# One transpose of x in place of two, with the row factors spread over the partitions

## The chip, the cores and the metric

The kernel runs on one core of a Trainium2 chip. The metric is device time in microseconds (us) of one execution; the time before is the median of 3 runs, 1371.86 us (1371.81 to 1372.82). In the profile PE is the matmul engine and PEld its weight loads, DVE, ACT and POOL are the vector, scalar and GpSimd engines, SP is the engine that issues the DMAs, and q behind an engine's name means its sequencer.

## The reference

One layer of a hybrid encoder: an adaLN-modulated RMSNorm, one wide input projection, sparse attention beside a Mamba-2 scan, a gated merge, and a SwiGLU feed-forward part. It is computed for 512 prompt rows and 64 sample rows of width 1024, 576 rows in all. What matters here is its very first step, and that x itself comes back at the first residual:

```python
mod = (jax.nn.silu(c) @ w_ada + b_ada)[:, None, :]
sh1, sc1, gt1, sh2, sc2, gt2 = jnp.split(mod, 6, axis=-1)
h = rms_normalize(x) * g_norm_mix * (1.0 + sc1) + sh1     # x * rsqrt(mean(x*x) + EPS) first
q, k, v, qi, ki, wi, z, xbc, dt, gate_logits = jnp.split(h @ w_in, offs, axis=-1)
...
x = x + gt1 * mixed
```

The shift and scale depend on the request group (prompt or sample) and on the channel; the factor 1/rms depends on the row.

## The kernel before

**How it is made.** The program is recorded, not issued at once: each call of `vec`, `act`, `pool`, `pe` or `sync` adds an operation to a plan (`Plan.add`, line 288), `Plan.order` (line 391) simulates all engines with a cost for each operation and takes, on each engine, the ready operation of the lowest priority number, and `Plan.emit` writes the operations out in that order. All instructions therefore carry the line of `emit`, 533; one goes by the names of the tiles. A block `with R.prio(n)` moves the priority of what is recorded in it. Each engine then works through its own list strictly in order, with semaphores between the lists.

**The layout.** The projection wants h with the channels on the partitions: `hTh` and `hTl`, 8 tiles of 128 channels x 576 rows each. They are the high and the low part of h, since every product is made of three fast fp32r matmuls (high x high, low x high, high x low). x comes in as five tiles `xt` with rows on the partitions, four of 128 rows and one of 64.

**The start, lines 802 to 893.** For each of the five tiles:

- ACT squares the tile into a scratch tile `xn` and sums the squares of each row into a column of `rs`. DVE multiplies by 1/1024 and adds EPS, POOL takes the power -1/2 (`rstd_of`). This gives the factor 1/rms of each row.
- DVE multiplies `xt` by the factor, into `xn` (two buffers).
- PE transposes the eight 128 x 128 blocks of `xn` into two PSUM tiles `px`, and ACT copies them to `xnT` (channels on partitions).
- Apart from that, PE transposes the eight blocks of the unscaled `xt` into a PSUM tile `mm` (two of them, two banks each), and DVE copies them to a tile `xs`. Six DMAs store these to `x_d` in DRAM, from where the first residual loads x much later. In the text this stands behind the making of h, with priority -1500.

So 40 blocks of `xn` and 40 blocks of `xt` are transposed.

**adaLN.** Four groups (`ada_pair`, j = 0 to 3) make shift and scale of 256 channels each. One needs four loads of 512 KB of `w_ada` (tiles `adr`, eight buffers, so that group j + 2 waits for the buffers of group j), 64 small matmuls into `py`, a copy `ra` on DVE, a transpose on PE, and the sums `modc` and `A` on DVE. `h_tile(kt)` then makes channel tile kt: `hu` = `xnT` * A + shift, on DVE for even kt and on ACT for odd kt, `hTh` is its rounded copy (ACT), `hTl` the rest (DVE, POOL for kt = 1 and 5):

```python
for j in range(4):
    ada_pair(j)
    fetch(0, EARLY[j])
    h_tile(2 * j)
    h_tile(2 * j + 1)
```

**Weights of the projection.** `fetch` loads slices of `w_in` into `raw` (two buffers); ACT makes the high part `wh`, DVE the low part `wl`, and a slice's buffer is loaded again when its `wl` is made. All these loads, those of `w_ada` and those of x stand in one list, SP's: the two small loads of c, the five of x, small rows, `w_ada` of group 0 (four), the first slice of `w_in` (the "misc" columns, in two pieces), `w_ada` of group 1, one slice, `w_ada` of group 2, two slices, `w_ada` of group 3, one slice. The first of the two slices between groups 2 and 3 goes into the buffer of the slice before group 2, so it waits for that one's `wl`.

**What PE does meanwhile.** As soon as channel tiles of h are there, PE begins the products of the first three slices (into `mm`, `px` and `py`), in pieces between the small matmuls of adaLN.

Of the kernel before, what the change touches and what calls it, by code (L numbers as in the profile page):

```python
# [5 lines left out]
F32 = mybir.dt.float32  # L6
F32R = mybir.dt.float32r
BF = mybir.dt.bfloat16
AF = mybir.ActivationFunctionType
OP = mybir.AluOpType  # L10
# [3 lines left out]
P = 128  # L14
D = 1024
NP_, NS = 512, 64
T = NP_ + NS
TH = T // 2
HP, HS = NP_ // 2, NS // 2
# [521 lines left out]
def build(tc, I, O):  # L541
    R = Plan(tc)
    vec, act, pool, pe, sync = R.vec, R.act, R.pool, R.pe, R.sync
# [5 lines left out]
    xsp = R.mkpool("xs", side="right")  # L549
    sp = R.mkpool("start")  # L550

    def pmm(name):
        return psum.tile([P, 2, 512], F32, name=name, tag="mm", bufs=2)

    def px(name, tag="px"):
        return psum.tile([P, 512], F32, name=name, tag=tag, bufs=2)
# [5 lines left out]
    ident = cp.tile([P, P], F32, name="ident")  # L562
# [129 lines left out]
    xt = []  # L692
    for tb in range(5):
        n = P if tb < 4 else NS
# [21 lines left out]
    sh1, sc1, gt1, sh2, sc2, gt2 = (modc[:, i] for i in range(6))  # L716
# [14 lines left out]
    def ada_pair(j):  # L731
# [15 lines left out]
        for w in range(2):  # L747
            vec.tensor_tensor(modc[:, w, 2 * j:2 * j + 2, :], p2[:, 64 * w:64 * w + 64].rearrange("p (g s) -> p g s", g=2)[:, :, 0:2],
                              badc[:, 8 * w + 2 * j:8 * w + 2 * j + 2, None].to_broadcast([P, 2, 2]), OP.add)
        vec.scalar_tensor_tensor(A1[:, 2 * j:2 * j + 2], sc1[:, 2 * j:2 * j + 2], 1.0, g_mix[:, 2 * j:2 * j + 2, None].to_broadcast([P, 2, 2]),  # L750
                                 op0=OP.add, op1=OP.mult)
# [39 lines left out]
    def rstd_of(ss, out, n, rows, denom):  # L791
        vec.tensor_scalar(out, ss, 1.0 / denom, EPS, op0=OP.mult, op1=OP.add)
        pow_mhalf(out, out, n)

    def bcast_rows(name, r5):

        pr = [px(name + "a"), px(name + "b", "py")]
        for tb in range(5):
            o = pr[0][:, tb * P:tb * P + P] if tb < 4 else pr[1][:, 0:P]
            pe.transpose(o, r5[:, tb:tb + 1].to_broadcast([P, P]), ident)  # L800
        return pr

    PARTS = ((0, 0, NP_), (1, NP_, NS))

    xnT = sp.tile([P, 8, T], F32, name="xnT")
    x_d = R.dram([P, 8, 2, TH], F32, name="x_d")
    rs = sp.tile([P, 5], F32, name="rs")
    pool.memset(rs, 1.0)
    for tb in range(5):
        n = P if tb < 4 else NS  # L810
        xn = sp.tile([P, D], F32, name=f"xn{tb}", tag="xn", bufs=2)
        act.activation(xn[:n], xt[tb][:n], AF.Square, accum_out=rs[:n, tb:tb + 1])
        rstd_of(rs[:n, tb:tb + 1], rs[:n, tb:tb + 1], 1, n, D)
        vec.tensor_scalar(xn[:n], xt[tb][:n], rs[:n, tb:tb + 1], None, op0=OP.mult)
        for k4 in range(2):
            p = px(f"pxn{tb}_{k4}")
            for j in range(4):
                kt = 4 * k4 + j
                pe.transpose(p[:, j * P:j * P + n], xn[:n, kt * P:(kt + 1) * P], ident[:n, :n])
            act.activation(xnT[:, 4 * k4:4 * k4 + 4, tb * P:tb * P + n], p.rearrange("p (k q) -> p k q", k=4)[:, :, :n], AF.Copy)  # L820
    rowsD = sp.tile([48, P], F32, name="rowsD")
    sync.dma_start(rowsD, I["b_ada"][0].rearrange("(a b) -> a b", b=P))
    badc = cp.tile([P, 48], F32, name="badc")
# [17 lines left out]
    stc = cp.tile([P, 3, 32], F32, name="stc")  # L841
    vec.tensor_scalar(bc_, vc[:, 32:64], 0.5, None, op0=OP.mult)

    A1 = cp.tile([P, 8, 2], F32, name="A1")
    hTh = hp.tile([P, 8, T], F32R, name="hTh")
    hTl = hp.tile([P, 8, T], F32R, name="hTl")
    hsS = hp.tile([P, 8, P], F32R, name="hsS")

    def h_tile(kt):
        u = sp.tile([P, T], F32, name=f"hu{kt}", tag="hu", bufs=3)  # L850
        for s, c0, n in PARTS:
            if kt % 2:
                act.activation(u[:, c0:c0 + n], xnT[:, kt, c0:c0 + n], AF.Identity, bias=sh1[:, kt, s:s + 1], scale=A1[:, kt, s:s + 1])
            else:
                vec.tensor_scalar(u[:, c0:c0 + n], xnT[:, kt, c0:c0 + n], A1[:, kt, s:s + 1], sh1[:, kt, s:s + 1], op0=OP.mult, op1=OP.add)
        act.activation(hTh[:, kt, :], u, AF.Copy)
        (pool if kt % 4 == 1 else vec).tensor_tensor(hTl[:, kt, :], u, hTh[:, kt, :].bitcast(F32), OP.subtract)

# [11 lines left out]
        act.activation(hsS[:, ks, 0:NS], hTh[:, ks, NP_:T].bitcast(F32), AF.Copy)  # L870
        act.activation(hsS[:, ks, NS:P], hTl[:, ks, NP_:T].bitcast(F32), AF.Copy)
    xst = []
    with R.prio(-1500):
        for tb in range(5):
            n = P if tb < 4 else NS
            p = pmm(f"pxt{tb}")
            for kt in range(8):
                pe.transpose(p[:, kt // 4, (kt % 4) * P:(kt % 4) * P + n], xt[tb][:n, kt * P:(kt + 1) * P], ident[:n, :n])
            st = xsp.tile([P, 8, P], F32, name=f"xs{tb}", tag="xs", bufs=5)
            for k4 in range(2):  # L880
                vec.tensor_copy(st[:, 4 * k4:4 * k4 + 4, :n], p[:, k4].rearrange("p (k q) -> p k q", k=4)[:, :, :n])
            if tb < 4:
                xst.append((x_d[:, :, tb // 2, tb % 2 * P:tb % 2 * P + P], st))
            else:
                for hf in range(2):
                    xst.append((x_d[:, :, hf, HP:TH], st[:, :, HS * hf:HS * hf + HS]))


    sync.dma_start(rowsB, I["w_conv"][0].rearrange("j (a b) -> (j a) b", b=P))
# [130 lines left out]
    p = px("pmiscT")  # L1020
# [3 lines left out]
    p = px("pmiscS")  # L1024
# [92 lines left out]
    p = px("pacs")  # L1117
# [11 lines left out]
    p = [px("pacsTa"), px("pacsTb", "py")]  # L1129
# [18 lines left out]
    for b in range(5):  # L1148
        n = P * (b + 1) if b < 4 else T
# [3 lines left out]
    for b in (4, 1, 2, 3):  # L1153
        smp = b == 4
        n = T if smp else P * (b + 1)
        rows = NS if smp else P
        k0 = NP_ if smp else 0
        s = ix.tile([P, n], F32, name=f"score{b}")
        for h in range(NIH // 2 if smp else NIH):
            q0 = 8 * NP_ + h * P if smp else h * NP_ + b * P  # L1160
            q = qis[:, q0:q0 + P]
# [101 lines left out]
    for kv in range(NKV):  # L1263
# [21 lines left out]
        for un in units + [None]:  # L1285
            nxt = None
            if un is not None:
                b, qs, k0, n, nk, v0, w = un
# [208 lines left out]
    for g in range(NG):  # L1497
# [4 lines left out]
        for i in range(4):  # L1502
# [9 lines left out]
            if 2 <= g < 6 and i > 1:  # L1512
                with R.prio(-600):
                    k = 2 * (g - 2) + i - 2
                    load_split(sd, o_d[:, k, :], oh[k], ol[k], 2)
    stage_c(NG - 1)
    for s, dst in ((0, O["conv_prompt"]), (1, O["conv_sample"])):
        p = px(f"pcvo{s}")
# [113 lines left out]
    for hf in range(2):  # L1632
# [4 lines left out]
        p = px(f"pss2{hf}")  # L1637
# [7 lines left out]
        pr = px(f"pr2{hf}", "py")  # L1645
# [175 lines left out]
    for i, (f, w, x, b, starts, *p) in enumerate(steps):  # L1821
# [198 lines left out]
    for o in order:  # L2020
        assert o in wd, o
        hi, lo = wd[o]
        if o[0] == "plain":
# [4 lines left out]
            for j in range(nk):  # L2028
                k = k0 + j
# [13 lines left out]
        else:  # L2043
            r, p = o[1:]
# [3 lines left out]
            bank_, q, starts = banks_d[r][b], DOWN[p][1], p in (1, 2, 7)  # L2048
# [49 lines left out]
```

## Time and profile before

| what | value |
|---|---|
| median of 3 runs | 1371.86 us |
| profiled execution: time, span | 1372.06 us, 1370.4 us |
| PE busy | 1351.5 us (99%) |
| PEld busy | 1312.5 us (96%) |
| DVE busy | 1112.8 us (81%) |
| ACT busy | 735.8 us (54%) |
| POOL busy | 250.8 us (18%) |
| moved by DMA | 200.70 MB, mean 146 GB/s |

The profiled execution is 0.2 us above the median of the runs, and 1.7 us of its time lie outside the span. A row of a timeline or chain gives the start and the duration in us, the engine, the operation with what it writes <- reads, and the number of instructions merged in the row; what stands in brackets is the idle time before it and what ended it. A row of windows gives, for a stretch of the span, its length, the busy time of each engine (with the number of instructions), the TensorE clock reported, the busy share of the DMA engines and the rate. A matmul's end is modelled, so the pace of PE is read from the distance of starts, not from the busy time.

### The profile page before, as it was taken

Reading aid. Unit: us, or ns where it says so; the run is one execution under the profiler, and the core shown is the slowest. Engines: PE = TensorE matmul, PEld = TensorE weight load, DVE = VectorE, ACT = ScalarE, POOL = GpSimd, SP = SyncE. Lnnn points to the kernel's source line nnn. Section 1 sums busy time; section 2 is a strip of 40 time slices with the busy share of each in tenths; the row PEclk is TensorE's granted clock in tenths of the full one; section 3 lists DMA queues with packets and bytes.
Section 4 is the critical chain, followed back from the end, with each engine's and each line's share of the span. In section 5 each row is a group of like instructions: output and inputs, shape, how many; then the busy total and the mean of one; then the engine's idle time right before and its main releaser. Section 6 shows DMA issues by size and latency. Waiting matters only on the chain.

```text
span 1370.4 us, 27779 instructions
## 1 busy us (share of the span) xinstructions
PE 1351.5 (99%) x10705; PEld 1312.5 (96%) x10705; DVE 1112.8 (81%) x2249; ACT 735.8 (54%) x1535; POOL 250.8 (18%) x376
## 2 busy tenths in 40 slices
PE   7999999999999999999999999999999999999998
PEld 5899999999999999999999999999999999999998
DVE  5688999787778698888897588868799998878564
ACT  5435343777876666666665342224576666664321
POOL 1312002230300245546453200001000000000000
PEclk9999999999999999999999999999999999999999
DMA  9762335574754644444445598757233343325431
GB/s 297 225 177 84 110 106 149 129 190 99 178 143 112 175 127 122 138 129 139 132 116 170 179 310 264 241 158 254 91 94 100 105 133 94 93 74 158 122 107 36
DMA packets 267764, 200.70 MB, mean 146 GB/s; under 512 B 25200, under 2 KB 239376, under 8 KB 267632
## 3 DMA queue, kind: packets, MB, share of 16 engines
q1 hardware_dynamic: 263680, 184.77, 46.0%
q0 software_dynamic: 3952, 14.16, 5.0%
q8 instruction: 84, 1.38, 0.4%
q14 instruction: 48, 0.39, 0.1%
HBM read 158.33 MB, written 29.55 MB: 137 GB/s over the span
## 4 chain that ended last, share of the span: by engine, by line
PE 86%; DVE 7%; DMA 4%; ACT 2%; issue 1%; SPq 1%; ACTq 0%; DVEq 0%
PE mm L533 61%; PE py L533 14%; PE px L533 11%; DMA stage<-y_d 2%; DVE score L533 1%; DMA raw<-in_w_in 1%; DVE m L533 1%; DVE wl L533 1%; SPq L533 1%; DMA xt<-in_x_sample 1%; DVE y L533 0%; ACT wh L533 0%; DVE xlS L533 0%; DMA rawu<-in_w_gate_up 0%; ACT wl L533 0%
## 5 line engine op out<-in xcount | busy, mean ns | idle before, releaser
L533 ACT ACTIVATE wh<-raw 128x1024 fp32r<-128x1024 f32 (+3 forms) x152 | 149.0, 983 | 181.4 <-PE mm L533 117.4
L533 PE MATMUL mm<-hTh,wh 128*128 128x288 f32 (+1 forms) x1024 | 235.5, 305 | 0.9 <-ACT hTh L533 0.9
L533 PE MATMUL mm<-hTh,wl 128*128 128x288 f32 (+1 forms) x1024 | 232.0, 301 | 0.0
L533 PE MATMUL mm<-hTl,wh 128*128 128x288 f32 (+1 forms) x1024 | 230.0, 301 | 0.4 <-DVE hTl L533 0.4
L533 PEld LDWEIGHTS mm<-hTh,wh 128*128 128x128 f32 (+1 forms) x1024 | 166.7, 188 | 3.9 <-ACT hTh L533 1.5
L533 PEld LDWEIGHTS mm<-hTh,wl 128*128 128x128 f32 (+1 forms) x1024 | 166.3, 188 | 2.7 <-issue 1.6
L533 PEld LDWEIGHTS mm<-hTl,wh 128*128 128x128 f32 (+1 forms) x1024 | 165.4, 188 | 3.3 <-issue 1.2
L533 DVE TENSOR_TENSOR wl<-raw,wh 128x1024 fp32r<-128x1024 f32 (+2 forms) x109 | 132.4, 1215 | 27.7 <-ACT wh L533 24.3
L533 DVE SCALAR_TENSOR_TENSOR cu<-xc,wc,cu 128x579 f32<-128x579 f32 x96 | 83.6, 870 | 2.1 <-ACT cu L533 1.6
L533 PE MATMUL mm<-wl,hTh 128*128 128x256 f32 x256 | 72.4, 284 | 0.0
L533 PE MATMUL mm<-wh,hTl 128*128 128x256 f32 x256 | 72.3, 284 | 0.0
L533 PE MATMUL mm<-wh,hTh 128*128 128x256 f32 x256 | 72.0, 284 | 0.0
L533 DVE SCALAR_TENSOR_TENSOR aacc<-adr,sil,aacc 128x512 f32<-128x512 f32 x84 | 59.8, 754 | 4.4 <-DMA adr<-in_w_ada 4.1
L533 PE MATMUL mm<-yh,wl 128*128 128x288 f32 x256 | 56.2, 298 | 0.0
L533 PE MATMUL mm<-yh,wh 128*128 128x288 f32 x256 | 55.2, 298 | 0.5 <-ACT yh L533 0.5
L533 PE MATMUL mm<-yl,wh 128*128 128x288 f32 x256 | 54.8, 296 | 0.6 <-DVE yl L533 0.6
L533 ACT ACTIVATE P<-lg,mn 128x128 f32<-128x128 f32 (+4 forms) x72 | 41.7, 581 | 25.2 <-DVE mn L533 24.0
L533 PE MATMUL mm<-xhS,wh 128*128 128x290 f32 (+1 forms) x248 | 55.2, 297 | 0.0
L533 PE MATMUL mm<-xhS,wl 128*128 128x290 f32 (+1 forms) x232 | 51.2, 296 | 0.0
L533 ACT ACTIVATE dec<-dec,nacs 128x128 f32<-128x128 f32 x128 | 42.5, 392 | 13.5 <-POOL dec L533 12.9
L533 PEld LDWEIGHTS mm<-wl,hTh 128*128 128x128 f32 x256 | 48.2, 189 | 0.4 <-issue 0.2
L533 PEld LDWEIGHTS mm<-wh,hTl 128*128 128x128 f32 x256 | 48.1, 188 | 0.3
(509 smaller groups left out, 3978.3 us busy)
## 6 DMA issues: line engine op xcount, KB each, us to landing
raw<-in_w_in SPq DMA_DIRECT2D x80, 512.0 KB, 4.0
adr<-in_w_ada SPq DMA_DIRECT2D x36, 512.0 KB, 5.2
raw<-in_w_gate_up SPq DMA_DIRECT2D x22, 512.0 KB, 3.8
wl<-raw POOLq DMA_DIRECT2D x21, 512.0 KB, 4.7
rawu<-in_w_gate_up SPq DMA_DIRECT2D x20, 512.0 KB, 3.9
bc<-acs_d SPq DMA_DIRECT2D x32, 256.0 KB, 3.6
raw<-in_w_branch_ssm SPq DMA_DIRECT2D x16, 512.0 KB, 4.5
raw<-in_w_down SPq DMA_DIRECT2D x16, 448.0 KB, 3.9
```

The costliest lines, as they stand in the source:

```text
L533: getattr(engines[x.eng], x.fn)(*[real(a) for a in x.args], **{k: real(v) for k, v in x.kw.items()})
```

## The change

x is transposed only once, unscaled, into `xT` (all 576 rows in one tile, in the pool that held `xs`). The squares go to a scratch tile `xsq` of one buffer. `bcast_rows` (line 795, which was there for another stage) transposes each column of `rs`, broadcast to 128 columns, on PE, so that every partition holds the 576 factors; ACT copies them from PSUM to `rB`. `h_tile` first multiplies the channel tile of `xT` by `rB`, on DVE, into `xr`. The six stores to `x_d` now read `xT`.

```diff
-    xnT = sp.tile([P, 8, T], F32, name="xnT")
+    xT = xsp.tile([P, 8, T], F32, name="xT")
+    xr = sp.tile([P, 8, T], F32, name="xr")
...
     for tb in range(5):
         n = P if tb < 4 else NS
-        xn = sp.tile([P, D], F32, name=f"xn{tb}", tag="xn", bufs=2)
-        act.activation(xn[:n], xt[tb][:n], AF.Square, accum_out=rs[:n, tb:tb + 1])
+        sq = sp.tile([P, D], F32, name=f"xsq{tb}", tag="xsq", bufs=1)
+        act.activation(sq[:n], xt[tb][:n], AF.Square, accum_out=rs[:n, tb:tb + 1])
         rstd_of(rs[:n, tb:tb + 1], rs[:n, tb:tb + 1], 1, n, D)
-        vec.tensor_scalar(xn[:n], xt[tb][:n], rs[:n, tb:tb + 1], None, op0=OP.mult)
+        p = pmm(f"pxt{tb}")
+        for kt in range(8):
+            pe.transpose(p[:, kt // 4, (kt % 4) * P:(kt % 4) * P + n], xt[tb][:n, kt * P:(kt + 1) * P], ident[:n, :n])
         for k4 in range(2):
-            p = px(f"pxn{tb}_{k4}")
-            for j in range(4):
-                kt = 4 * k4 + j
-                pe.transpose(p[:, j * P:j * P + n], xn[:n, kt * P:(kt + 1) * P], ident[:n, :n])
-            act.activation(xnT[:, 4 * k4:4 * k4 + 4, tb * P:tb * P + n], p.rearrange("p (k q) -> p k q", k=4)[:, :, :n], AF.Copy)
+            vec.tensor_copy(xT[:, 4 * k4:4 * k4 + 4, tb * P:tb * P + n], p[:, k4].rearrange("p (k q) -> p k q", k=4)[:, :, :n])
...
+    pr = bcast_rows("prx", rs)
+    rB = sp.tile([P, T], F32, name="rB")
+    act.activation(rB[:, 0:NP_], pr[0], AF.Copy)
+    act.activation(rB[:, NP_:T], pr[1][:, 0:NS], AF.Copy)
...
     def h_tile(kt):
+        vec.tensor_tensor(xr[:, kt], xT[:, kt], rB, OP.mult)
         u = sp.tile([P, T], F32, name=f"hu{kt}", tag="hu", bufs=3)
...
-                vec.tensor_scalar(u[:, c0:c0 + n], xnT[:, kt, c0:c0 + n], A1[:, kt, s:s + 1], sh1[:, kt, s:s + 1], op0=OP.mult, op1=OP.add)
+                vec.tensor_scalar(u[:, c0:c0 + n], xr[:, kt, c0:c0 + n], A1[:, kt, s:s + 1], sh1[:, kt, s:s + 1], op0=OP.mult, op1=OP.add)
...
-    with R.prio(-1500):
-        for tb in range(5):
-            n = P if tb < 4 else NS
-            p = pmm(f"pxt{tb}")
-            for kt in range(8):
-                pe.transpose(p[:, kt // 4, (kt % 4) * P:(kt % 4) * P + n], xt[tb][:n, kt * P:(kt + 1) * P], ident[:n, :n])
-            st = xsp.tile([P, 8, P], F32, name=f"xs{tb}", tag="xs", bufs=5)
-            for k4 in range(2):
-                vec.tensor_copy(st[:, 4 * k4:4 * k4 + 4, :n], p[:, k4].rearrange("p (k q) -> p k q", k=4)[:, :, :n])
-            if tb < 4:
-                xst.append((x_d[:, :, tb // 2, tb % 2 * P:tb % 2 * P + P], st))
-            else:
-                for hf in range(2):
-                    xst.append((x_d[:, :, hf, HP:TH], st[:, :, HS * hf:HS * hf + HS]))
+    for tb in range(4):
+        xst.append((x_d[:, :, tb // 2, tb % 2 * P:tb % 2 * P + P], xT[:, :, tb * P:tb * P + P]))
+    for hf in range(2):
+        xst.append((x_d[:, :, hf, HP:TH], xT[:, :, NP_ + HS * hf:NP_ + HS * hf + HS]))
```

More of the change, by code (lines that the diff above doesn't have):

```diff
@@ L852, in h_tile @@
             if kt % 2:
-                act.activation(u[:, c0:c0 + n], xnT[:, kt, c0:c0 + n], AF.Identity, bias=sh1[:, kt, s:s + 1], scale=A1[:, kt, s:s + 1])
+                act.activation(u[:, c0:c0 + n], xr[:, kt, c0:c0 + n], AF.Identity, bias=sh1[:, kt, s:s + 1], scale=A1[:, kt, s:s + 1])
             else:
-                vec.tensor_scalar(u[:, c0:c0 + n], xnT[:, kt, c0:c0 + n], A1[:, kt, s:s + 1], sh1[:, kt, s:s + 1], op0=OP.mult, op1=OP.add)
+                vec.tensor_scalar(u[:, c0:c0 + n], xr[:, kt, c0:c0 + n], A1[:, kt, s:s + 1], sh1[:, kt, s:s + 1], op0=OP.mult, op1=OP.add)
         act.activation(hTh[:, kt, :], u, AF.Copy)
```

## The prediction

> **What bounds the kernel now.** I read the page first, then the busy time in windows of 5 us, then the timeline, chain and waits of the first 50 us, the only place that the change touches.
>
> ```profile
> PE 1351.5 (99%) x10705; PEld 1312.5 (96%) x10705; DVE 1112.8 (81%) x2249; ACT 735.8 (54%) x1535; POOL 250.8 (18%) x376
> ```
>
> ```profile
> core 0: us, PE busy (x) PEld busy (x) DVE busy (x) ACT busy (x) POOL busy (x), PEclk, DMA share, GB/s
> 5.00:10.00 5.00, 3.83 (x17) 3.44 (x18) 2.17 (x5) 2.30 (x4) 0.64 (x2) 1.00 1.02 347
> 15.00:20.00 5.00, 3.77 (x53) 2.93 (x54) 3.18 (x8) 3.04 (x6) 1.10 (x2) 1.00 1.14 290
> 25.00:30.00 5.00, 3.68 (x46) 2.77 (x47) 1.63 (x5) 3.04 (x5) 1.41 (x1) 1.00 1.13 331
> 35.00:40.00 5.00, 4.46 (x53) 3.63 (x52) 2.30 (x7) 2.09 (x4) 0.00 (x0) 1.00 1.13 335
> 55.00:60.00 5.00, 5.00 (x44) 5.00 (x43) 4.29 (x11) 1.88 (x3) 1.53 (x2) 1.00 1.00 300
> ```
>
> PE is the bound: 19 us of the span are not PE's, and most of them lie in the first 45 us, where its windows hold 3.7 to 4.5 of 5 us. From 50 us on it is full, so what arrives there late or early by 1 us moves the end by 1 us. In the first 40 us it is the DMA engines that are full (share 1.02 to 1.14). Who waits for whom there:
>
> ```profile
> 5.38 1.54 PE L533 MATMUL mm<-ident,xt 128*128 128x128 f32 x6 [2.32 <-DMA xt<-in_x_prompt]
> 6.96 0.69 DVE L533 COPY xs<-mm 128x512 f32<-128x512 f32 x1 [3.14 <-PE mm L533]
> 7.71 3.04 PE L533 MATMUL mm<-ident,xt 128*128 128x128 f32 x13 [0.78 <-DVE rs L533]
> 13.71 1.04 PE L533 MATMUL px<-ident,xn 128*128 128x128 f32 x8
> 22.04 0.28 DVE L533 COPY ra<-py 128x128 f32<-128x128 f32 x1
> 22.34 1.02 DVE L533 TENSOR_TENSOR wl<-raw,wh 128x832 fp32r<-128x832 f32 x1
> 24.62 0.77 DVE L533 TENSOR_SCALAR hu<-xnT,A,modc 128x512 f32<-128x512 f32 x2
> 26.45 0.26 PEld L533 LDWEIGHTS mm<-hTh,wh 128*104 128x104 f32 x2 [0.81 <-ACT hTh L533]
> 27.82 1.07 PE L533 MATMUL py<-adr,sil 128*32 128x128 f32 x28
> 28.94 0.29 DVE L533 COPY ra<-py 128x128 f32<-128x128 f32 x1 [1.75 <-PE py L533]
> 29.81 1.23 DVE L533 TENSOR_TENSOR wl<-raw,wh 128x1024 fp32r<-128x1024 f32 x1 [0.58 <-ACT wh L533]
> 31.07 0.92 SPq L533 DMA_DIRECT2D raw<-in_w_in  x2
> 32.08 4.86 SPq L533 DMA_DIRECT2D adr<-in_w_ada  x4
> 37.41 0.43 PE L533 MATMUL mm<-hTh,wl 128*128 128x288 f32 x2
> 44.18 0.80 PEld L533 LDWEIGHTS py<-adr,sil 128*32 128x32 f32 x28 [0.18 <-DMA adr<-in_w_ada]
> 48.61 2.12 DVE L533 TENSOR_TENSOR hTl<-hu,hTh 128x576 fp32r<-128x576 f32 x2 [0.44 <-ACT hTh L533]
> 50.78 0.26 PEld L533 LDWEIGHTS mm<-hTl,wh 128*104 128x104 f32 x2 [0.42 <-DVE hTl L533]
> ```
>
> The stage ends when the last tiles of h are ready (48.61 to 50.73, PE waits for them at 50.78). They hang on the last load of the fourth w_ada group, which releases PE at 44.18. So what decides is when that load lands, not how soon x is transposed. Two rows of the chain and one of the page's list of issues tell how much air its queue has:
>
> ```profile
> 3.43 7.62 DMA xt<-in_x_sample
> 31.49 6.56 DMA raw<-in_w_in
> ...
> raw<-in_w_in SPq DMA_DIRECT2D x80, 512.0 KB, 4.0
> ```
>
> The slice issued at 31.49 lands at 38.05, 6.56 us later, against 4.0 us typical of such a load. It is the second of two issued together, and at some 340 GB/s (windows) the 512 KB ahead of it take 1.5 us. So 6.56 - 4.0 - 1.5 = 1.1 us of queue stand in front: the issue at 31.07 may come 1.1 us later before anything lands later; beyond that the delay reaches the four w_ada loads behind it, one for one.
>
> **The change, part by part.** As built, SP's list has the same loads in the same order. The lists of the other engines differ only up to the products and sums of w_ada's second group (about 30 us in the trace), apart from names. The six stores to x_d keep their place and their chunks of 512 and 128 bytes per row: 0.
>
> ```profile
> L533 PE MATMUL px<-ident,xn x40: 222/272/421, 10.5 to 22.7; 128*128 128x128 f32 x32, 64*128 64x64 f32 x8
> L533 ACT ACTIVATE xnT<-px x10: 378/594/598, 11.6 to 23.0; 128x512 f32<-128x512 f32 x8, 128x256 f32<-128x256 f32 x2
> L533 ACT ACTIVATE xn<-xt x5: 1047/1057/1057, 5.4 to 19.4; 128x1024 f32<-128x1024 f32 x4, 64x1024 f32<-64x1024 f32 x1
> L533 ACT ACTIVATION_READ_ACCUMULATOR xn<-xt x5: 187/190/202, 6.4 to 20.3; 128x1 f32 x4, 64x1 f32 x1
> L533 DVE TENSOR_SCALAR xn<-xt,rs x5: 743/745/754, 9.0 to 21.4; 128x1024 f32<-128x1024 f32 x4, 64x1024 f32<-64x1024 f32 x1
> L533 DVE COPY xs<-mm x10: 414/686/692, 7.0 to 17.6; 128x512 f32<-128x512 f32 x8, 128x256 f32<-128x256 f32 x2
> 33.23 1.43 DVE L533 TENSOR_TENSOR hTl<-hu,hTh 128x576 fp32r<-128x576 f32 x2 [1.04 <-ACT hTh L533]
> 7.80 0.57 POOL L533 TENSOR_TENSOR rs<-rs,mhalf 128x1 f32<-128x1 f32 x1 [5.55 <-DVE rs L533]
> ```
>
> Removed: 40 transposes on PE, 10 ACT copies (8 x 0.59 + 2 x 0.38 = 5.5 us) and 5 DVE products (5 x 0.75 = 3.7 us). Added: 5 transposes, two ACT copies (0.6 and some 0.25 us), 8 DVE products of 576 columns. The nearest row for these is hTl, also two SBUF operands of 576 columns: 1.43 us for two, so 5.7 us for eight. The ten DVE copies stay. DVE has 2 us more work and ACT about 4.7 us less, both far from full there. What counts is the chain, in which three things get later:
>
> 1. *The blocks of x.* A block of x used to be interleaved with transposes of xn. Now four of them follow each other, and in each the last two transposes wait until DVE has copied the first bank, as in the first block before: six from 5.38, copy 6.96 to 7.65, the rest from 7.71. PE's pace in these rows is (3.04 - 0.42) / 12 = 0.22 us a transpose at first and (1.04 - 0.27) / 7 = 0.11 from 13 us on, though the clock is given as 1.00 throughout (0.42 and 0.27 are the duration of one in each row). A block is 7.71 + 2 x 0.21 - 5.38 = 2.75 us at the slow pace, about 1.9 at the fast one. Four blocks from 5.38: 15.4 us if the pace doubles at 13.0 as before, 16.4 if it stays slow; the sample's half block and two small transposes: 16.0 or 17.5. x itself has long landed (11.05 by the chain), and the last of the five squares, 1.06 us and 0.19 for reading the sum, is done by 12.3.
>
> 2. *The factors.* All five must be there before any tile of h. The fifth stands on DVE behind the copies (16.0 or 17.2), POOL adds 0.57, then five transposes, an ACT copy of 0.6 and their handovers: 18.3 or 20.0. Then eight products, 5.7 us, which DVE does before `ra` of w_ada's first group: until 24.0 or 25.7. Before, `ra` was at 22.04. `ra`, the low part of the misc slice (1.0 us), `modc` and `A` follow: `hu` at 25.6 or 27.3, against 24.62.
>
> 3. *Who waits.* PE stands behind the transpose of `ra`, so the second group's matmuls queue there, though their data is in. `ra` of the second group comes at about 29.9 (before 28.94). If PE is still slow, then at about 32.8: `hu` at 27.3, 1.8 us to PE's first product (24.62 to 26.45), then 8 products and 32 small matmuls at twice their time. Products start 0.13 us apart (0.43 us for two of 0.30), the small ones 0.8 / 28 = 0.029 (1.07 us less the 0.27 of one), so 2.0 and 1.8 us. DVE makes the low part `wl` of the first full slice behind it, 1.23 us, and SP's issue of 31.07 waits for that: 31.4 or 34.3.
>
> The sum: 31.4 is 0.3 late, less than the 1.1 us of queue, so 0. 34.3 is 3.2 late, so 3.2 - 1.1 = 2.1 us reach the last w_ada load, the tiles of h and the end. If the pace doubles on the way, in the 20s, I get `ra` some 1.8 us late, with 0.7 us left over. Before shows both paces and one change between them, after some 5 us of nearly unbroken work; it does not show how PE behaves with a block's pauses of about 1 us. In the changed kernel an unbroken run comes only with the small matmuls of group 1 (64, about 20 to 23 us) or with the products from 27 on. I take +1.0 us, between these two. By the saved work nothing is gained: PE's 35 passes, ACT's copies and DVE's products all fall before 44 us, under the loads.
>
> [...]
>
> **The rivals.**
>
> *Faster: the transposes were on the path.* 35 passes fewer at 0.11 us are 3.8 us: 1371.86 - 3.8 = 1368.1 us. PE's fullness over the whole span speaks for it. Against it: PE waits for loads at 44.18, and the loads' order and bytes don't change. It would need DMA time to shrink.
>
> *Slower: the slow pace lasts into the full stage.* From 36 us on PE has hardly any idle time, and each us at half pace loses 0.5 us beside the 2.1. It decides, past 0.2%, if the pace doubles later than about 38 us; at 44 us it would be 2.1 + 0.5 x 8 = 6.1 us at most, less PE's idle time in the 35 to 40 window (0.5): about 5.5 us, 1377.4 us. For it: long pauses before 28 us. Against it: PE has unbroken work from 28 on, and before, 5 us of it were enough.
>
> *Nothing at all.* The pace doubles at 13 us as before, the queue's air takes up the 0.3 us: 1371.9 us.
>
> **How the numbers follow.** A measurement of this kernel can hardly tell less than 0.2% (2.7 us) from no change. Forecast, 0 to 2.1 us slower with the likeliest +1.0: 1372.9 us (its span by the profile 1371.4; the profiled execution took 1372.06, 0.2 above the median). Chance of the forecast with "nothing at all", which is its lower end: 0.84. Slower rival, of which I put the most just past 0.2%: 0.12. Faster rival: 0.04. The range: 1371.2 below (nothing at all, less what the runs scatter), 1374.9 above, 0.9 past the sum at slow pace, for the start of the slower rival. The same cases give faster 0.04, same 0.84, slower 0.12.
>
> **What would show it.** Right: PE's first transposes in blocks with pauses for DVE; eight `xr` products, one after the other, near 18 to 26 us; the first `hu` at 25 to 27.5; SP's pair of slices at 31.4 to 34.3; the release of PE by the last w_ada load at 44 to 46.3, and the wait for `hTl` at 50.8 to 52.9; the order and pace behind that as before. Wrong: if that load lands before 43.5 (a gain that I exclude); if `wl` of the first slice is past 35; if the stage after 53 us takes another time than before; or if transposes to strided rows of `xT` make DVE's copies longer than 0.69 us, at 0.1 us each 1 us more in step 2.

## The result, and the profile after

| | before | changed |
|---|---|---|
| median of the runs made together (8 each) | 1372.88 us (1371.81 to 1374.21) | 1377.32 us (1375.72 to 1378.77) |
| ratio, 95% interval | | 1.0032 (1.0021 to 1.0042) |
| profiled execution: time, span | 1372.06 us, 1370.4 us | 1377.31 us, 1375.5 us |

The change makes the kernel 4.4 us slower, and its time lies 2.4 us past the upper end of the range predicted (the kernel before, measured beside it, is 1.0 us above the median from which the forecast starts). The interval of the ratio lies clear of 1. PE's and DVE's busy times are within 1.3 us of what they were. From the page of the changed kernel, its first part:

```profile
PE 1352.2 (98%) x10670; PEld 1311.5 (95%) x10670; DVE 1114.1 (81%) x2252; ACT 732.5 (53%) x1527; POOL 250.8 (18%) x376
```

So the span has 4.4 us more in which PE isn't busy (23.3 us against 18.9). The windows of the changed kernel show where (length, busy time of PE, PEld, DVE, ACT and POOL, the granted clock, DMA share, GB/s):

```profile
20.00:25.00 5.00, 3.35 (x64) 2.70 (x56) 4.55 (x7) 1.20 (x2) 0.00 (x0) 1.00 1.10 344
25.00:30.00 5.00, 2.30 (x37) 1.47 (x39) 3.86 (x10) 2.60 (x5) 0.23 (x1) 0.73 1.12 332
30.00:35.00 5.00, 5.00 (x45) 3.81 (x46) 0.86 (x2) 0.63 (x1) 1.18 (x1) 0.59 0.50 160
35.00:40.00 5.00, 5.00 (x71) 3.73 (x73) 3.07 (x8) 3.13 (x6) 0.00 (x0) 1.00 0.69 190
40.00:45.00 5.00, 4.33 (x50) 3.47 (x39) 2.93 (x8) 2.62 (x4) 0.00 (x0) 1.00 1.11 340
```

Two things are new. DVE is all but full from 20 to 25 us (4.55 of 5), and PE idles and then works at a granted clock of 0.73 and 0.59 until 35 us; before, the clock stood at 1.00 here. And the DMA engines, which were full to 40 us, fall to shares of 0.50 and 0.69 between 30 and 40. The timeline of the changed kernel has the chain:

```profile
10.36 1.97 PE L533 MATMUL mm<-ident,xt 128*128 128x128 f32 x8 [0.79 <-DVE rs L533]
13.11 1.97 PE L533 MATMUL mm<-ident,xt 128*128 128x128 f32 x8 [0.78 <-DVE rs L533]
19.71 3.64 PE L533 MATMUL py<-adr,sil 128*32 128x128 f32 x64
20.45 5.44 DVE L533 TENSOR_TENSOR xr<-xT,rB 128x576 f32<-128x576 f32 x8 [1.41 <-ACT rB L533]
25.81 0.28 DVE L533 COPY ra<-py 128x128 f32<-128x128 f32 x1
26.24 0.30 PE L533 MATMUL py<-ident,ra 128*128 128x128 f32 x1 [2.88 <-DVE ra L533]
27.40 0.77 DVE L533 TENSOR_SCALAR hu<-xr,A,modc 128x512 f32<-128x512 f32 x2
29.17 0.81 PE L533 MATMUL mm<-hTh,wh 128*104 128x288 f32 x2 [1.46 <-ACT hTh L533]
34.14 0.29 DVE L533 COPY ra<-py 128x128 f32<-128x128 f32 x1 [4.24 <-PE py L533]
34.35 1.22 DVE L533 TENSOR_TENSOR wl<-raw,wh 128x1024 fp32r<-128x1024 f32 x1
35.59 0.92 SPq L533 DMA_DIRECT2D raw<-in_w_in  x2
48.49 1.07 PE L533 MATMUL py<-adr,sil 128*32 128x128 f32 x28
53.11 2.11 DVE L533 TENSOR_TENSOR hTl<-hu,hTh 128x576 fp32r<-128x576 f32 x2
```

Follow one delay through them. DVE makes all eight `xr` before the first `ra`, which is at 25.81 in place of 22.04. PE waits 2.88 us for it. The trace's record of the granted clock begins with full pace at 23.84, when the 64 small products of 19.71 to 23.35 have ended, and has half pace from 27.25 and full pace again from 34.08 us. Ahead of 23.84 there is no record, so the 1.00 of the window from 20 us is no reading of the pace. The second `ra` comes at 34.14 in place of 28.94 (5.2 us late), `wl` behind it, SP's slices at 35.59 in place of 31.07 (4.5), PE's last small products of w_ada at 48.49 in place of 44.18 (4.3), the last tiles of h at 53.11 in place of 48.61 (4.5). From there both profiles run in step, 4.6 us apart, until 456 us. Between 456 and 502 us another 1.7 us come, and 1.1 us go again after 750 us, which I haven't explained: 5.1 us of span.

### The profile page after: what moved, and what is told of

It reads as the page before. It is cut to its first block, busy times and chain, and to the rows that moved or that the text cites. A ratio compares the mean times of both kernels' runs of the same rounds, so it can differ in the third digit from the quotient of the medians.

```text
span 1375.5 us, 27695 instructions
## 1 busy us (share of the span) xinstructions
PE 1352.2 (98%) x10670; PEld 1311.5 (95%) x10670; DVE 1114.1 (81%) x2252; ACT 732.5 (53%) x1527; POOL 250.8 (18%) x376
## 4 chain that ended last, share of the span: by engine, by line
PE 87%; DVE 6%; DMA 3%; ACT 2%; issue 1%; SPq 0%; POOL 0%; ACTq 0%; POOLq 0%; DVEq 0%
PE mm L533 61%; PE py L533 15%; PE px L533 11%; DVE score L533 1%; DVE m L533 1%; DMA stage<-y_d 1%; DVE wl L533 1%; DMA raw<-in_w_in 0%; DVE cu L533 0%; ACT wh L533 0%; DMA bc<-acs_d 0%; DMA stage<-o_d 0%; DVE xr L533 0%; DMA rowsC<-in_state_conv 0%; ACT wl L533 0%
## 5 line engine op out<-in xcount | busy, mean ns | idle before, releaser
L533 ACT ACTIVATE P<-lg,mn 128x128 f32<-128x128 f32 (+4 forms) x72 | 41.8, 581 | 25.5 <-DVE mn L533 24.3
L533 PEld LDWEIGHTS mm<-wl,hTh 128*128 128x128 f32 x256 | 48.2, 189 | 0.4 <-issue 0.2
```

The source lines that it names most:

```text
L533: getattr(engines[x.eng], x.fn)(*[real(a) for a in x.args], **{k: real(v) for k, v in x.kw.items()})
```

## The experiments

In the edits below the lists that the plan has ordered are altered before they are written out: `put` moves an operation in its engine's list, `extra` makes a new one, `find` names one by engine and tile. All else stays. As a mark for the state of the first stage I take when the store of `out_v_prompt` is issued, 119.29 us in the first profile before; the last column is what the distance to that profile grows by between 456.76 us (the store to `o_d`) and 502.44 us (the first store of `out_ssm_sample`).

| run | median us | kernel before beside it | ratio (95%) | mark, late by | 456 to 502 us |
|---|---|---|---|---|---|
| changed | 1377.32 | 1372.88 | 1.0032 (1.0021 to 1.0042) | 4.61 | +1.70 |
| e11, changed again | 1378.90 | 1372.98 | 1.0041 (1.0028 to 1.0053) | 5.38 | +1.52 |
| e10, before again | 1372.89 | 1372.98 | 0.9997 (0.9989 to 1.0006) | 1.53 | 0.00 |
| e1, xr in turn | 1374.62 | 1373.13 | 1.0013 (1.0005 to 1.0022) | 1.05 | +0.53 |
| e9, before + five products | 1376.17 | 1372.98 | 1.0021 (1.0012 to 1.0030) | 4.04 | 0.00 |
| e3, PE kept busy | 1376.22 | 1373.13 | 1.0023 (1.0010 to 1.0036) | 2.19 | 0.00 |
| e4, first try at a late slice | 1377.62 | 1373.13 | 1.0034 (1.0022 to 1.0046) | 5.85 | 0.00 |
| e5, before, slice late | 1377.29 | 1372.58 | 1.0036 (1.0023 to 1.0048) | 5.77 | 0.00 |
| e2, one slice behind w_ada | 1376.74 | 1373.13 | 1.0027 (1.0016 to 1.0038) | 4.05 | +1.41 |
| e6, changed, slices last | 1378.05 | 1372.58 | 1.0042 (1.0028 to 1.0055) | 4.70 | +2.00 |
| e8, before, slices last | 1372.61 | 1372.58 | 1.0003 (0.9994 to 1.0012) | -0.41 | 0.00 |
| e7, xr in turn, slices last | 1375.08 | 1372.58 | 1.0016 (1.0007 to 1.0025) | 0.90 | +1.59 |
| e12, e7 + banks | 1374.52 | 1372.98 | 1.0007 (0.9999 to 1.0016) | 0.06 | +0.85 |
| e13, changed + banks | 1378.82 | 1372.98 | 1.0033 (1.0021 to 1.0044) | 5.46 | +2.38 |
| e14, e7 + 36 instructions | 1376.11 | 1373.10 | 1.0022 (1.0007 to 1.0037) | 1.35 | 0.00 |
| e15, changed + 36 instructions | 1377.52 | 1373.10 | 1.0034 (1.0020 to 1.0049) | 4.05 | 0.00 |

**Is it DVE's order? e1 and e9.** My theory after the result was that everything follows from DVE's eight products standing ahead of `ra`. e1 leaves the work and moves six of them:

```diff
+ xr = [self.find("vector", "xr", kt) for kt in range(8)]
+ for g, behind in ((1, "hu0"), (2, "hu3"), (3, "hu4")):
+     last = self.find("vector", "hTl", 0, behind)
+     self.put(xr[2 * g + 1], after=last)
+     self.put(xr[2 * g], after=last)
```

> The changed kernel with one list altered, DVE's: only the two xr products of the first two channel tiles stand ahead of the first ra; the other six are made pair by pair, each pair behind the hTl of the group before. Theory (DVE's eight products hold ra up, the rest follows from that): the first ra at about 23.5 us instead of 25.81, SP's pair of slices issued at 31.5 to 33.5 instead of 35.59, the last w_ada load releases PE 2 to 4 us earlier than in the changed kernel; time +0.3 to +2 us against the kernel before, 1373 to 1375 where the changed kernel takes 1377.3. Rival (the loss is in the work that was added or in x's blocks, not in its order): within 1 us of the changed kernel.

The timeline of e1:

```profile
20.45 1.43 DVE L533 TENSOR_TENSOR xr<-xT,rB 128x576 f32<-128x576 f32 x2 [1.41 <-ACT rB L533]
22.86 0.29 DVE L533 COPY ra<-py 128x128 f32<-128x128 f32 x1 [0.98 <-PE py L533]
24.45 0.77 DVE L533 TENSOR_SCALAR hu<-xr,A,modc 128x512 f32<-128x512 f32 x2
29.45 0.28 DVE L533 COPY ra<-py 128x128 f32<-128x128 f32 x1
32.16 0.92 SPq L533 DMA_DIRECT2D raw<-in_w_in  x2
```

The first `hu` is now earlier than in the kernel before (24.45 against 24.62), the clock rises once, at 22.0 us, and stays. The mark is 1.05 us late in place of 4.61. In this profile the loads of w_ada were themselves 1.0 to 1.5 us late from 17 us on, before the moved products could tell; in e12, the same DVE list without such a delay, the mark is 0.06 late. Over the four profiles with this list (e1, e7, e12, e14) it is 0.06 to 1.35 late, no more than the kernel before in its own second profile (e10, 1.53); over the six with the eight products in one row it is 4.05 to 5.46 (e3, which also keeps PE busy, apart). So the order carries the loss of the first stage, as far as these marks can tell.

e9 goes the other way. It adds DVE products alone to the kernel before:

```diff
+ ra, x = self.find("vector", "ra0"), self.find("vector", "xn3").args[1].base.view()
+ spare = self.find("vector", "xn3").args[0].base.view()
+ for i in range(5):
+     self.put(self.extra("vector", "tensor_tensor", spare[:, 0:T], x[:, 0:T], x[:, 0:T], OP.mult), before=ra)
```

> The kernel before with five products of 128x576 added on DVE right ahead of the first ra (the first x tile by itself, into a scratch tile that nothing reads): some 3.5 us, so that the first ra comes at about 25.6 us as in the changed kernel, while PE has been at full pace since 12 to 13 us and x is transposed as before. Theory (DVE's work ahead of ra is the whole cause): PE idles about 3 us, its clock falls, the second ra comes at 33 to 34.5, the time rises by 4 to 5 us to about 1377. Rival (the new order of x's transposes and the late warming of PE have a share of their own): 1 to 2.5 us above the kernel before.

The timeline of e9:

```profile
21.33 3.91 DVE L533 TENSOR_TENSOR xn<-xt 128x576 f32<-128x576 f32 x5
25.16 0.28 DVE L533 COPY ra<-py 128x128 f32<-128x128 f32 x1
25.50 0.48 PE L533 MATMUL py<-ident,ra 128*128 128x128 f32 x1 [3.27 <-DVE ra L533]
33.34 0.29 DVE L533 COPY ra<-py 128x128 f32<-128x128 f32 x1 [3.00 <-PE py L533]
34.79 0.92 SPq L533 DMA_DIRECT2D raw<-in_w_in  x2
```

PE had been at full pace since 11.6 us, and x was transposed as ever. The first `ra` at 25.16 is enough for the rest: half pace from 25.26 to 35.5, the second `ra` at 33.34, the mark 4.04 us late. The time rose by 3.2 us, between the 4 to 5 of the theory and the 1 to 2.5 of the rival, with no loss later. Its mark is 0.6 to 1.3 us less late than in the two profiles of the changed kernel. Its first `ra`, 0.65 us earlier, may account for that much; a share of up to 0.7 us for the order of x's transposes and the late rise of the clock is not excluded.

**How much of it is the clock? e3.** PE gets 36 transposes that nothing reads, where it waits for `ra` and for the first product:

```diff
+ for op, n in ((turn, 24), (first, 12)):
+     for i in range(n):
+         self.put(self.extra("tensor", "transpose", spare, turn.args[2], turn.args[2]), before=op)
```

> The changed kernel with 36 transposes of the identity into unused columns of a PSUM tile added on PE: 24 ahead of the transpose of the first ra, 12 ahead of the first product of the projection. Their results are not read. DVE's order stays, so the first ra stays at 25.8. Theory with the clock as the second cause: the granted clock does not fall at 27 us, the second ra comes 2 to 3 us earlier than 34.14, and the time is 2 to 3 us below the changed kernel's, 1374.3 to 1375.3. Rival (the late first ra alone accounts for the loss): the second ra within 0.7 us of 34.14 and the time within 1 us of the changed kernel's, or above it.

The windows of e3:

```profile
25.00:30.00 5.00, 5.00 (x67) 4.04 (x66) 3.78 (x10) 2.30 (x4) 0.30 (x1) 1.00 1.12 335
30.00:35.00 5.00, 5.00 (x77) 4.10 (x79) 2.50 (x7) 2.23 (x4) 1.13 (x1) 1.00 0.93 275
```

Its timeline:

```profile
31.98 0.29 DVE L533 COPY ra<-py 128x128 f32<-128x128 f32 x1 [2.13 <-PE py L533]
33.43 0.92 SPq L533 DMA_DIRECT2D raw<-in_w_in  x2
```

The first `ra` is as late as in the changed kernel (25.73), the clock stays at 1.00, the second `ra` comes at 31.98 (2.2 us earlier than 34.14), and the mark is 2.4 us better. So by these profiles about half of the stage's loss is the late `ra` and about half the half pace that follows from PE's wait for it. By the time the gain is 1.1 us, less than the 2 to 3 expected, and the runs scatter widely (1373.1 to 1381.0 us); the last group of experiments has part of the reason.

**Does it reach the end through the loads? e4, e5, e2, e6.** The chain that I had predicted went through SP: `wl` late, the slices' loads late, the loads of w_ada behind them late. e4 was to delay SP's wait alone, in the kernel before, by making the first full slice's `wl` once more behind the second group's `hTl`.

```diff
+ wl1 = self.find("vector", "wl1")
+ self.put(self.extra("vector", wl1.fn, *wl1.args, **wl1.kw), after=self.find("vector", "hTl", 0, "hu3"))
```

> The kernel before with one operation more: DVE makes the low part wl of the first full slice a second time, behind the hTl of the second group, where DVE is idle (34.66 to 35.9 us). Nothing else is late; only SP's wait for the slice's buffer ends about 4.8 us later, at 35.9 as in the changed kernel. Theory (the wait on SP's list is the path): the loads behind land 4 to 5 us later and the time rises by 4 to 5 us over the kernel before, to about 1377. Rival (PE's pace or DVE's work carries the loss): within 1 us of the kernel before. By the 1.1 us of queue that I had taken, +3.7; by 0.2 us, +4.6.

It did something else. The new operation stood behind the next slice's load in the program, so it waited for that load and overwrote `wl` with values of the wrong slice. DVE stood until 38.6 and PE until 39.8 us, and its 4.5 us say nothing of SP. e5 does what was meant: it reads the slice into a scratch tile, and the loads are issued behind it.

```diff
+ again = self.extra("vector", wl1.fn, spare, *wl1.args[1:], **wl1.kw)
+ self.put(again, after=last)
+ loads = [self.find("sync", n) for n in ("raw3", "raw2", "wada300", "wada301", "wada310", "wada311")]
+ for op in reversed(loads):
+     self.put(op, after=again)
```

> The kernel before with one operation more on DVE, in a gap: behind the hTl of the second group (34.66 us) it reads the first full slice once more, into a scratch tile that nothing reads, and the next load into that slice's buffer is issued behind it. PE, ACT and DVE have nothing else late by it; only SP's wait ends at about 36 us in place of 31.07, as in the changed kernel. Theory (SP's wait alone carries the loss): the loads behind land 4 to 5 us later, the time is 4 to 5 us above the kernel before. Rival (the loads have more air than that, or PE alone carries the loss): 0 to 1 us above.

The timeline of e5:

```profile
34.50 1.22 DVE L533 TENSOR_TENSOR xn<-raw,wh 128x1024 f32<-128x1024 f32 x1
35.80 0.92 SPq L533 DMA_DIRECT2D raw<-in_w_in  x2
41.71 1.06 ACT L533 ACTIVATE wh<-raw 128x1024 fp32r<-128x1024 f32 x1 [6.61 <-DMA raw<-in_w_in]
42.82 0.61 PE L533 MATMUL px<-hTh,wh 128*128 128x288 f32 x1 [4.25 <-ACT wh L533]
```

Late loads alone cost 4.7 us: the way through SP is a real one. The pair's second slice landed 3.6 us later for an issue 4.7 us later, so there was 1.1 us of queue, as I had taken it. PE then waited 4.25 us for the slice and lost its clock (half pace from 41.3 to 48.2). In this execution it had been at half pace from 24.3 to 27.7 us too, ahead of the edit; that has no share in the delay of the loads, since the new operation began on time, at 34.50.

But it isn't the only way. e2 and e6 take the wait out of the changed kernel. In e2 the load that waits for `wl` goes behind w_ada's fourth group, in e6 both slices that wait go behind the small rows too:

```diff
+ self.put(self.find("sync", "raw3"), after=self.find("sync", "wada311"))      # e2
+ slices = self.find("sync", "raw3", 0), self.find("sync", "raw3", 1)          # e6
+ self.put(slices[1], after=self.find("sync", "rowsC"))
+ self.put(slices[0], before=slices[1])
```

> The changed kernel with one list altered, SP's: of the two slices between the third and fourth w_ada group, the one that waits for wl is issued behind the fourth group. PE, DVE and ACT keep their lists, so ra stays late and PE cold. Theory (the loss reaches the end through SP's wait, which lets the DMA queue run dry): the windows 30 to 40 us are full again (DMA share above 1), the fourth group's loads land at least 4 us earlier than in the changed kernel, and the time is that of the kernel before or up to 2 us less, 1371 to 1373. Rival (the half pace of PE between 27 and 34 us costs the time itself, whatever the loads do): within 1.5 us of the changed kernel, 1376 to 1378.

> The changed kernel with SP's list altered further than in e2: the two loads into the slices' buffers that wait for a wl stand behind the fourth w_ada group and the small rows (dt_bias to state_conv), so that nothing that PE needs stands behind a wait for wl. DVE, PE and ACT keep their lists: ra late, PE cold until about 34 us. If PE's own list is as late as the loads were (what e2 suggests): PE has no idle time between 30 and 50 us, the stage ends 3 us later than before, 1375.5 to 1376.5. If the loads alone carry the loss: the time of the kernel before or less, 1372 to 1373.5.

The windows of e6:

```profile
30.00:35.00 5.00, 5.00 (x42) 3.73 (x42) 0.76 (x3) 0.79 (x1) 1.33 (x1) 0.50 1.14 328
35.00:40.00 5.00, 5.00 (x55) 3.90 (x55) 3.31 (x8) 3.19 (x7) 0.00 (x0) 0.91 1.11 343
```

Its timeline:

```profile
48.56 1.07 PE L533 MATMUL py<-adr,sil 128*32 128x128 f32 x28
```

The DMA engines are full again, and the last load of the fourth group lands at 42.3 us, 6 us before PE comes to use it at 48.56, the very time at which it came in the changed kernel (48.49). In e2 PE comes to it at 47.38 and then waits 0.93 us for small rows that SP issued behind its next wait. My theory of the loads fell here: the loads were early and the time stayed (e6 came out 1.5 us above what I had expected even for that case; 2.0 us of its loss lie between 456 and 502). PE's own list is as late, by the 2.9 us of waiting (3.4 in e6) and the half pace until 34 or 36 us, and it is full behind that.

**Are both ways equally long in the kernel before? e8.** The same edit as e6's, in the kernel before:

> The kernel before with SP's list as in e6 alone. If the loads of the fourth w_ada group set the end of its first stage, as I had argued, the 512 KB ahead of them taken away let them land 1.5 us earlier: 1 to 1.5 us less, 1371.5 to 1372.2. If PE's list is the limit as well: within 0.7 us of the kernel before.

The timeline of e8:

```profile
43.43 0.80 PEld L533 LDWEIGHTS py<-adr,sil 128*32 128x32 f32 x28 [0.18 <-issue]
43.43 1.07 PE L533 MATMUL py<-adr,sil 128*32 128x128 f32 x28
47.86 2.48 DVE L533 TENSOR_TENSOR hTl<-hu,hTh 128x576 fp32r<-128x576 f32 x2 [0.50 <-ACT hTh L533]
```

The row at 43.43 no longer waits for a load (the last one landed at 42.85), and the stage ends 0.4 us earlier, not 1.5. The time is that of the kernel before. PE's list was within half a microsecond of the loads all along.

**What is left with a mended start? e7, e12, e13.** e7 joins e1 and e6:

> The changed kernel with DVE's list as in e1 (xr in turn) and SP's as in e6. Neither limit is late then: the fourth group's loads land 1.5 us earlier than in e1, and PE is warm from about 22 us. Theory: at or up to 1.5 us below the kernel before, 1371.5 to 1373.5. Rival (the added work itself costs): 1374 or more.

The mark is 0.90 late, but the time 2.5 us above the kernel before, since 1.6 us are lost between 456 and 502 us. There the lists are the same in all kernels. I noticed that the changed kernel takes its first PSUM tile from `mm`, so that `px` and `mm` swap banks, and turned that back, with the mended start (e12) and without (e13):

```diff
+ ps = self.find("tensor", "pxt0").args[0].base.pool
+ ps.tags = {k: ps.tags[k] for k in ("py", "px", "mm")}
```

> e7 (xr in turn, waiting slices last) with the PSUM tiles placed as in the kernel before: since the first tile that the changed kernel takes is mm and no longer px, its px and mm stand in each other's banks throughout; here their order is turned back. If the banks cause the loss of 1 to 2 us that the profiles of the changed kernel and of e1, e2, e6 and e7 show between 456 and 502 us: no growth there, and the time 1 to 2 us below e7's, 1373 to 1374. If not: 1.5 us again in that stretch, the time as e7's, about 1375.

> The changed kernel with the PSUM tiles placed as in the kernel before, nothing else. First stage as in the changed kernel (SP's pair of slices at 35 to 36 us). If the banks cause the later loss: none of it between 456 and 502 us, the time 1.5 us below the changed kernel's, about 1376.5. If not: as the changed kernel, 1377.5 to 1379.

e13 lost 2.4 us in that stretch, and e12 still 0.85: it isn't the banks. e12 is the best kernel with one transposition, 1.0007 (0.9999 to 1.0016), not to be told from the kernel before.

**The loss at 456 to 502 us: e14, e15.** The table has a pattern. The stretch costs nothing in the kernels with the old start and in e3, and 0.5 to 2.4 us in all others; e3 has 36 PE instructions more, and the new start has 35 fewer than the old. Each of these transposes is two instructions, a weight load and a product. The trace shows what depends on their number: the fetches of the instructions themselves, which also go over the DMA engines. The DMA view of the kernel before, 471 to 473 us, where hardly anything else is moved:

```profile
DMA packets 4, 0.02 MB, mean 9 GB/s; under 512 B 1, under 2 KB 3, under 8 KB 3
## 3 DMA queue, kind: packets, MB, share of 16 engines
q8 instruction: 1, 0.02, 2.9%
```

One packet of 16 KB (1.38 MB in 84 packets over the whole profile) takes 2.9% of 16 engines in 2 us, so 0.93 us of one engine. In the kernel before it starts at 471.7 us and meets no one. In the changed kernel the fetch starts at 483.2 and in e7 at 479.8, among the loads of `o_d`, where the 16 engines are full (share 1.00 to 1.14 in e7 from 477.78 to 480.78). Counted in the time of the kernel before, it lies between 471.5 and 471.8 us in all nine profiles without growth, and between 478.1 and 479.7 in all eight with it. That the loads wait for the engine which the fetch holds is an inference; no view here shows the engines one by one. e14 and e15 add 36 small transposes to e7 and to the changed kernel, while PE waits for the first x:

```diff
+ first = self.find("tensor", "pc")
+ spare = first.args[0].base.view()[0:16, 128:144]
+ for i in range(36):
+     self.put(self.extra("tensor", "transpose", spare, first.args[2], first.args[2]), after=first)
```

> e7 (xr in turn, waiting slices last) with 36 small transposes (16x16, of the identity, results not read) on PE while it waits for the first x. The new start has 35 PE instructions fewer, so that the fetches of PE's instructions (16 KB each, 0.9 us on one DMA engine) stand some 7 us later in the rest of the program: in the kernel before and in e3 (which has 36 more) one lies at about 472 and 476 us, where the queue is idle, in the others at 478 to 485 us, among the loads of o_d. If that makes the loss between 456 and 502 us: the fetch is back at about 472 us, no growth there, and the time 1 to 1.5 us below e7's, at the kernel before, 1372.5 to 1374. If not: growth as in e7 (1.6 us) and 1375.

> The changed kernel with the same 36 small transposes, nothing else. Its first stage stays late or a little less so (PE may be at full pace some us earlier: the second ra between 32 and 34 us). If the fetches make the later loss: no growth between 456 and 502 us, the time 1.5 us below the changed kernel's, 1375.5 to 1377. If not: as the changed kernel.

The DMA views of e7 (from 474.78 us) and of e14 (from 474.08 us), each over the same 12 us of work; the last column of an issue's row is the median from issue to landing:

```profile
q8 instruction: 1, 0.02, 0.5%
...
stage<-o_d SPq DMA_DIRECT2D x4, 288.0 KB, 4.7
```

```profile
stage<-o_d SPq DMA_DIRECT2D x4, 288.0 KB, 3.8
```

In e14 the fetch starts at 473.0 us, is gone from the window, and the loads take 3.8 us, as in the kernel before (3.7 in its 12 us). The growth is gone in both, e15 included (9.47 us late at 456 and 9.47 at 502). So the place of the fetches makes this loss, in the profiles. But the times did not fall as expected: e14's runs go from 1372.3 to 1381.4 us, their median 1.0 above e7's, and e15's median is that of the changed kernel. e15's profile shows another loss, made from 232 to 261 us: a load of `kstd` took 8.9 us (7.05 before), and PE stood and lost its clock:

```profile
250.00:255.00 5.00, 1.83 (x14) 1.59 (x12) 1.92 (x5) 4.04 (x9) 1.54 (x1) 0.92 0.68 208
255.00:260.00 5.00, 4.97 (x22) 4.97 (x23) 4.37 (x11) 2.96 (x8) 2.88 (x2) 0.50 0.34 65
```

e3, which has 36 more as well, lost 1.4 us at the same place. In e15 and e3 a fetch starts 3.0 and 2.0 us later than in the kernel before (where it is at 232.1 us), in the midst of that load; in e14, which lost nothing here, it is at its old place. So it may be the same mechanism; no run tests it.

**Both kernels again: e10, e11.**

> The kernel before once more, unchanged: its first stage as in the first profile (SP's pair of slices issued at 31 to 32), and the part from 460 to 510 us for comparison. Within 0.1% of itself.

> The changed kernel once more, unchanged: SP's pair of slices at 35 to 36 us, 4 to 5 us above the kernel before. If the further 1.7 us between 460 and 500 us come from the change, they stand in this profile too; if they are scatter of a load, not.

The windows of e10, the kernel before:

```profile
25.00:30.00 5.00, 4.51 (x48) 3.15 (x50) 2.08 (x7) 2.29 (x4) 1.42 (x1) 0.50 1.04 314
```

Its timeline:

```profile
24.38 0.64 PE L533 MATMUL py<-adr,sil 128*32 128x128 f32 x4 [2.07 <-DMA adr<-in_w_ada]
32.91 0.92 SPq L533 DMA_DIRECT2D raw<-in_w_in  x2
```

In this execution a load of w_ada came 3.4 us late, PE waited 2.07 us, and the kernel before, too, ran at half pace from 24.4 to 31.2 us. It ended 1.5 us later than in its first profile. So part of the scatter of the kernel before (1370.7 to 1374.9 us in these runs) is the same mechanism, set off by a load; the changed kernel's list sets it off in each of its six profiles, the variants included. e4 and e5 lost the pace as well, at 24 to 26 us, ahead of their edits, and so did e14, with the mended list: there a load of w_ada landed 2.9 us late, and half pace lasted 3.41 us, from 25.3. e11 repeats the first profile after: slices at 35.67, mark 5.4 late, 1.5 us more from 456 to 502.

## Why the prediction was wrong

**Step 1, the blocks of x: right.** They follow each other 2.75 us apart (7.61, 10.36, 13.11), at the slow pace, and the copies to `xT` stay at 0.69 us.

**Step 2, the factors: right, in its slow case.** The eight products begin at 20.45 (20.0 said), take 5.44 us (5.7) and end at 25.9 (25.7), the first `hu` is at 27.40 (27.3), PE's first product at 29.17 (29.1).

**Step 3, who waits: the mechanism right, two terms too small.** PE stands behind `ra`, SP behind `wl`, w_ada behind the slices, as told. The slow case had the second `ra` at 32.8; it came at 34.14. I had counted 8 products and 32 small ones at twice their time, 3.8 us, and dropped the handovers between them. The whole stretch doubles, handovers and all: from 26.45 to 28.94 us it was 2.49 us before, from 29.17 to 34.14 it is 4.97. That is 1.2 us. The second term is the queue's air. Taken as 1.1 us, it was 1.1 and 1.2 in e5 and e9, but 0.2 and 0.0 in the two profiles of the changed kernel, where a load of the pair took longer. 2.1 + 1.2 + 0.9 is 4.2 us, against the 4.3 measured at the last small products of w_ada. So the upper end of the forecast, 2.1, was itself half of what came.

**The sum: the step that failed.** Between no delay and 2.1 us I took +1.0, on the ground that the pace might double "on the way, in the 20s". It did, at 23.84 us, half a us after the 64 small products had ended; but PE stood still for `ra` by then, and the pace was gone again at 27.25. I had both pieces, the pace that had doubled in the kernel before at 13.0 us, after 5.29 us in which PE was never idle (from 7.71), and the wait of 2 us and more that DVE's products make, and did not put the one into the other: with a wait for `ra` of 2.88 us here and of 3.27 us in e9 the pace was lost again, whenever it had been gained (in e9 it was gained at 11.6 us and lost at 25.26). By e3 that is 2.2 us of the second `ra`. So two things failed: the choice of +1.0, which needed the pace to stay, and behind it the two terms of step 3, which leave even the slow case, +2.1, 2.3 us short of the 4.4 measured.

**"What decides is when that load lands": half the truth.** It missed that PE's list is full as well, once the first products begin. e6 gave the loads back and kept the loss; in e8 the last load landed 1.3 us before the 44.18 of the kernel before, which gained 0.4 us of the stage and nothing of the time. The row at 44.18 had shown it: its idle time, 0.18 us, is what the same row has in e8, where it waits for no load. In the windows of before one could have seen it: from 30 to 50 us PE idles 1 us in all, so of what PE loses ahead of 30 us no more than that could be made good.

**The rivals.** The slower one's 1377.4 us is near the measured time by luck: it needed the pace to double later than 38 us, and the pace was back before 36. Its ground, that each us at half pace costs PE half a us once it is full, fits from about 29 us on, not from 36: from 29.17 to 34.08 it gives 2.5 us, and e3 measured 2.2. The faster one had nothing for it; e12, where hardly anything is late in the first stage, is not faster than the kernel before.

**After the first stage** I expected the same time as before, and 0.5 us net came on top in the first profile (5.1 of span less 4.6). The 1.7 us of it between 456 and 502 are, by e14 and e15, the fetches of instructions, of which nothing in the prediction spoke; the 1.1 us that go again after 750 stay open.

## What to carry to other kernels

Where an engine's list is strictly in order, work that is ready early is not free: six products that nobody needed yet stood ahead of one small copy, and moving them behind it took nearly all of the first stage's loss away (the mark 0.06 to 1.35 us late in place of 4.05 to 5.46). Price a wait of the matmul engine by the clock that it may take with it (2.2 us of the second `ra` by e3), and price a stretch at half pace by doubling the whole stretch of the trace, handovers included (2.49 us became 4.97). When a wait for a load ends last by a hair, test the engine's own list by giving the load back before calling the load the bound.

## What was not expected of the hardware

In the records of the granted clock of these runs, within the span, half pace came in pieces of 3.41 (e14), 6.83 (the changed kernel, from 27.25 us) and 10.24 us (e9, from 25.26), and full pace between two of half pace, or ahead of the first, in pieces of 3.41 (the changed kernel, from 23.84 us), 6.83 (e4), 13.65 (e9) and once, in e15, 218.45 us: all whole multiples of 3.41 us. PE was not without work when it lost the pace: in the 3.41 us ahead of the drop it was busy for 1.01 us in the changed kernel and 1.17 in e10, whose longest waits were 2.88 and 2.07 us. What decides it these runs don't show: e5 lost the pace after 3.41 us with 2.09 us of work, e12 kept it after 3.41 us with 1.72.

The count of instructions on PE moved the fetches of instructions in the rest of the program. The DMA views of the whole profile before and of that after, each with this row for the queue (packets, MB, share):

```profile
q8 instruction: 84, 1.38, 0.4%
```

```profile
q8 instruction: 83, 1.36, 0.4%
```

The kernel before has 10705 products on PE and as many weight loads. If the 84 packets are all PE's, the 21410 instructions are 255 to a packet; for it speaks that e14, which differs from e7 in PE's list alone, has its fetch at 473.0 us in place of 479.8. The changed kernel has 35 of both fewer, so 70 instructions, and by that count every later fetch moves by more than a quarter of its distance to the next. The one at 471.7 us moved to 478.6 in the time of the kernel before, where the next one had been at 492.2. A fetch of 16 KB took 0.93 us of one DMA engine, and where it fell among the loads of `o_d`, with the engines full (shares of 1.00 to 1.14 in e7), these landed 0.9 us later (4.7 in place of 3.8 us). So a fetch had a cost in these runs to the loads beside it.
